# Expert dispatch: weights loaded in 1 KB runs and put in tile order by block transposes, first input tile loaded by strided partition sets

## The chip, the core and the metric

The kernel runs on one core of a Trainium2 chip. The metric is the device time of one execution in microseconds, as the median of several runs. One execution was also profiled, and its trace is what the prediction reads.

## What is computed

Each token's row of 512 numbers is written twice, once times each of the token's two expert weights. The expert indices are an input that the result does not use.

```python
batch, seq, hidden, k = 16, 1024, 512, 2
x_expanded = x[:, :, np.newaxis, :].repeat(k, axis=2)
return (x_expanded * expert_weights[..., np.newaxis]).astype(np.float32)
```

All is float32: 33.55 MB of x and 0.13 MB of weights are read, 67.11 MB are written.

## The kernel before

The 16384 tokens are taken in 8 tiles of 2048. In a tile, partition p holds 16 tokens that follow one another in memory, so that one partition's row of x is 16 x 512 numbers, 32 KB in one run. Tiles of x go through a pool of two buffers, output tiles through a pool of four.

**Weights.** One SBUF tile `w_tile` of 128 x 256 holds all of them: column (tile x 16 + token) x 2 + expert. It is filled by eight DMAs on SP's queue (lines 54 and 55), one for each tile of x; each writes 32 numbers, 128 bytes, to each of 128 partitions.

**Loads of x.** `load(i)` (lines 69 to 77) issues one DMA of 4 MB on ACT's queue, of 128 rows of 32 KB (line 76). Tiles 0 and 1 are loaded ahead of the loop. Tile i+2 is loaded after the compute of tile i, into the buffer that tile i leaves; it waits until DVE and ACT have read that.

**Compute.** For each of the 16 tokens of a partition, DVE multiplies 128 x 512 by the first weight (line 97) and ACT by the second (line 91). The weight is a column of `w_tile`, one number per partition.

**Stores.** After every 8 tokens SP issues one DMA of 4 MB (line 105), of 128 rows of 32 KB. There are 16 of them. Weight loads and stores stand in one queue (SP's, q1 in the profile), loads of x in another (ACT's, q10).

The order of the work is that of the program on each engine and queue. Waits on tiles are put in by the framework. It also shares out eight semaphores among the DMAs in turn, so that a DMA can wait for an older one that used the same semaphore: the second load of x waits for the first weight load, the eighth weight load for the first load of x, and the first stores for weight loads.

Of the kernel before, what the change touches and what calls it, by code (L numbers as in the profile page):

```python
# [1 line left out]

# [4 lines left out]


@with_exitstack
def kernel(  # L10
    ctx: ExitStack,
    tc: tile.TileContext,
    x: bass.AP,
    expert_indices: bass.AP,
    expert_weights: bass.AP,
    out: bass.AP,
):
    nc = tc.nc

    batch, seq, hidden = x.shape  # L20
    k = expert_weights.shape[-1]
    P = nc.NUM_PARTITIONS
    ntok = batch * seq
    assert ntok % P == 0
    A_TOTAL = ntok // P

    f32 = mybir.dt.float32
    row = k * hidden
    TX = 16
    TO = 8  # L30


    groups = [[16], [16], [16], [16], [16], [16], [16], [16]]
    assert sum(sum(g) for g in groups) == A_TOTAL

    xf = x.rearrange("b s h -> (b s) h")
    of = out.rearrange("b s k h -> (b s) (k h)")
    wf = expert_weights.rearrange("b s k -> (b s) k")

    w_pool = ctx.enter_context(tc.tile_pool(name="w_pool", bufs=1))  # L40
    x_pool = ctx.enter_context(tc.tile_pool(name="x_pool", bufs=2))
    o_pool = ctx.enter_context(tc.tile_pool(name="o_pool", bufs=4))

    w_tile = w_pool.tile([P, A_TOTAL * k], f32)

    def rows(of_all, done, T):
        return of_all[done * P : (done + T) * P, :].rearrange(
            "(p a) n -> p (a n)", a=T
        )

    weights = []
    for group in groups:
        weights.append((sum(n for _, n in weights), sum(group)))
    for at, T in weights:
        nc.sync.dma_start(out=w_tile[:, at * k : (at + T) * k], in_=rows(wf, at, T))

    tiles = []
    done = 0
    for group in groups:
        T = sum(group)  # L60
        a0 = 0
        for n in group:
            tiles.append((done, T, a0, n))
            a0 += n
        done += T

    loaded = []

    def load(i):
        if i >= len(tiles):  # L70
            return
        done, T, a0, n = tiles[i]
        x_tile = x_pool.tile([P, TX * hidden], f32)
        cols = rows(xf, done, T)[:, a0 * hidden : (a0 + n) * hidden]
        for lo, hi in [(0, P)]:
            nc.scalar.dma_start(out=x_tile[lo:hi, : n * hidden], in_=cols[lo:hi, :])  # L76
        loaded.append(x_tile)

    for i in range(2):
        load(i)  # L80
    for i, (done, T, a0, n) in enumerate(tiles):
        x_tile = loaded[i]
        outr = rows(of, done, T)
        for t in range(n):
            if t % TO == 0:
                o_tile = o_pool.tile([P, TO * row], f32)
            for kk in range(k):
                c = (done + a0 + t) * k + kk
                o = t % TO * row + kk * hidden
                if kk == 1:  # L90
                    nc.scalar.mul(  # L91
                        out=o_tile[:, o : o + hidden],
                        in_=x_tile[:, t * hidden : (t + 1) * hidden],
                        mul=w_tile[:, c : c + 1],
                    )
                    continue
                nc.vector.tensor_scalar(  # L97
                    out=o_tile[:, o : o + hidden],
                    in0=x_tile[:, t * hidden : (t + 1) * hidden],
                    scalar1=w_tile[:, c : c + 1],  # L100
                    scalar2=None,
                    op0=mybir.AluOpType.mult,
                )
            if (t + 1) % TO == 0:
                nc.sync.dma_start(
                    out=outr[:, (a0 + t + 1 - TO) * row : (a0 + t + 1) * row],
                    in_=o_tile,
                )
        load(i + 2)

# [1 line left out]
_INS = ['x', 'expert_indices', 'expert_weights']  # L112
_OUTS = [((16, 1024, 2, 512), 'float32')]


# [23 lines left out]
```

## Time and profile before

| | us |
|---|---|
| median of 11 runs | 240.28 |
| lowest and highest run | 240.06, 241.75 |
| profiled execution, its own time | 241.75 |
| its span in the trace | 240.0 |
| DVE busy | 51.9 (128 multiplies of 480 ns) |
| ACT busy | 81.3 (128 multiplies of 708 ns, one table load of 1283 ns) |
| first load of x, issue to landing | 12.8 |
| first weight load, issue to landing | 3.0 |
| all eight weight loads, median to landing | 21.7 |

The profile's page gives the span in 40 slices of 6 us with the share of DMA time and the GB/s of each slice; the busy time of each engine; the DMAs by the line that issues them; and groups of instructions with what ended the idle time before them. The trace can be asked for the same by windows of any length. It also holds a record of every DMA packet: when it began, how long it took, its bytes and its queue, but not its DMA engine; where the prediction speaks of single engines, packets were put in 16 chains, each packet behind the one that ended just before it.

The profile's whole-kernel figures are 100.81 MB moved in 240.0 us, 420 GB/s on average.

### The profile page before, as it was taken

Reading aid. Unit: us, or ns where it says so; the run is one execution under the profiler, and the core shown is the slowest. Engines: PE = TensorE matmul, PEld = TensorE weight load, DVE = VectorE, ACT = ScalarE, POOL = GpSimd, SP = SyncE. Lnnn points to the kernel's source line nnn. Section 1 sums busy time; section 2 is a strip of 40 time slices with the busy share of each in tenths; the row PEclk is TensorE's granted clock in tenths of the full one; section 3 lists DMA queues with packets and bytes.
Section 4 is the critical chain, followed back from the end, with each engine's and each line's share of the span. In section 5 each row is a group of like instructions: output and inputs, shape, how many; then the busy total and the mean of one; then the engine's idle time right before and its main releaser. Section 6 shows DMA issues by size and latency. Waiting matters only on the chain.

```text
span 240.0 us, 384 instructions
## 1 busy us (share of the span) xinstructions
DVE 51.9 (22%) x128; ACT 81.3 (34%) x129; POOL 0.2 (0%) x4
## 2 busy tenths in 40 slices
DVE  0073810055005005050040502205041135000000
ACT  2079870085207108071170802508044165200000
POOL 0000000000000000000000000000000000000000
DMA  6999999999999999999999999999999999999994
GB/s 265 439 433 364 438 437 437 432 437 426 432 426 415 418 415 426 426 437 437 432 432 432 426 437 432 426 426 432 437 437 437 437 437 437 437 432 437 437 432 197
DMA packets 4610, 100.81 MB, mean 420 GB/s; under 512 B 1536, under 2 KB 1536, under 8 KB 1536
## 3 DMA queue, kind: packets, MB, share of 16 engines
q1 hardware_dynamic: 3456, 67.24, 65.2%
q10 hardware_dynamic: 1152, 33.55, 33.2%
q14 instruction: 2, 0.02, 0.0%
HBM read 33.69 MB, written 67.11 MB: 420 GB/s over the span
## 4 chain that ended last, share of the span: by engine, by line
DMA 48%; another core or an unknown queue 21%; ACT 16%; ACTq 1%; issue 1%
DMA out_dram<-o_tile 38%; ACT o_tile L91 16%; DMA x_tile<-in_x_dram 9%; DMA w_tile<-in_expert_weights_dram 1%; ACTq L76 1%; ACTq L134 0%; ACTq L91 0%
## 5 line engine op out<-in xcount | busy, mean ns | idle before, releaser
L91 ACT ACTIVATE o_tile<-x_tile,w_tile 128x512 f32<-128x512 f32 x128 | 80.0, 708 | 120.0 <-DMA out_dram<-o_tile 97.0
L97 DVE TENSOR_SCALAR o_tile<-x_tile,w_tile 128x512 f32<-128x512 f32 x128 | 51.9, 480 | 151.9 <-DMA out_dram<-o_tile 116.5
L91 ACT ACT_TABLE_LOAD x1 | 1.3, 1283 | 4.2 <-DMA w_tile<-in_expert_weights_dram 4.2
L123 POOL MEMSET const-bfloat16-1.0<- 128x1 bf16 x1 | 0.1, 102 | 0.0
L123 POOL MEMSET const-uint8-127<- 128x1 uint8 x1 | 0.1, 102 | 0.0
L123 POOL MEMSET const-float32-0.0<- 128x1 f32 x1 | 0.1, 99 | 0.2 <-issue 0.2
L123 POOL MEMSET const-float32-1.0<- 128x1 f32 x1 | 0.1, 99 | 0.0
## 6 DMA issues: line engine op xcount, KB each, us to landing
out_dram<-o_tile SPq DMA_DIRECT2D x16, 4096.0 KB, 48.7
x_tile<-in_x_dram ACTq DMA_DIRECT2D x8, 4096.0 KB, 23.1
w_tile<-in_expert_weights_dram SPq DMA_DIRECT2D x8, 16.0 KB, 21.7
```

The lines of the kernel that those rows point to most:

```text
L76: nc.scalar.dma_start(out=x_tile[lo:hi, : n * hidden], in_=cols[lo:hi, :])
L91: nc.scalar.mul(out=o_tile[:, o : o + hidden], in_=x_tile[:, t * hidden : (t + 1) * hidden], mul=w_tile[:, c : c + 1],)
L97: nc.vector.tensor_scalar(out=o_tile[:, o : o + hidden], in0=x_tile[:, t * hidden : (t + 1) * hidden], scalar1=w_tile[:, c : c + 1], scala ...
L123: nc = _bacc.Bacc("TRN2", target_bir_lowering=False, num_devices=1)
```

## The change

**Weights.** One DMA on SP's queue reads all weights in memory order: 128 rows of 256 numbers, 1 KB each, into `w_in`. In that order partition p holds the weights of tokens 128p to 128p + 127. Two steps on DVE bring them into the tile order of before: a transpose of the 32 x 32 blocks of the whole 128 x 256 tile into `w_mid`, then 16 transposes of 32 partitions x 64 numbers, which read `w_mid` with strides and write the blocks of `w_tile` at their partitions.

**First tile of x.** It is loaded by four DMAs on ACT's queue, of partitions 0, 8, 16, ... (16 rows), 4, 12, 20, ... (16 rows), 2, 6, 10, ... (32 rows) and 1, 3, 5, ... (64 rows). All other tiles are loaded as before.

The loops over groups of tiles are written out for the one group length in use; multiplies and stores are the same in number, shape and order. With fewer DMAs at the start, the second load of x waits for no weight load any more. ACT's table load, which came after a wait for the first weight load, now comes after a wait for the four DMAs of the first tile.

```diff
-    wf = expert_weights.rearrange("b s k -> (b s) k")
+    wf = expert_weights.rearrange("b s k -> (b s k)")
...
-    w_tile = w_pool.tile([P, A_TOTAL * k], f32)
...
-    for at, T in weights:
-        nc.sync.dma_start(out=w_tile[:, at * k : (at + T) * k], in_=rows(wf, at, T))
...
+    w_in = w_pool.tile([P, R * C], f32)
+    w_mid = w_pool.tile([P, R * C], f32)
+    w_tile = w_pool.tile([P, G * C], f32)
+    nc.sync.dma_start(out=w_in, in_=wf.rearrange("(p n) -> p n", p=P))
+    nc.vector.transpose(out=w_mid, in_=w_in)
+    GQ = G // (P // B)
+    for dst in range(P // B):
+        for src in range(P // B):
+            nc.vector.transpose(
+                out=w_tile[
+                    dst * B : (dst + 1) * B, src * GQ * C : (src + 1) * GQ * C
+                ],
+                in_=w_mid[src * B : (src + 1) * B, :].rearrange(
+                    "c (q g h j) -> c g h j q", q=R, g=GQ, h=P // B
+                )[:, :, dst],
+            )
...
     def load(i):
-        if i >= len(tiles):
+        if i >= G:
             return
-        done, T, a0, n = tiles[i]
         x_tile = x_pool.tile([P, TX * hidden], f32)
-        cols = rows(xf, done, T)[:, a0 * hidden : (a0 + n) * hidden]
-        for lo, hi in [(0, P)]:
-            nc.scalar.dma_start(out=x_tile[lo:hi, : n * hidden], in_=cols[lo:hi, :])
+        if i == 0:
+            for at, step in ((0, 8), (4, 8), (2, 4), (1, 2)):
+                nc.scalar.dma_start(
+                    out=x_tile[at::step, :], in_=rows(xf, i)[at::step, :]
+                )
+        else:
+            nc.scalar.dma_start(out=x_tile, in_=rows(xf, i))
         loaded.append(x_tile)
```

Here P = 128, B = 32, G = 8 tiles, C = 32 weights of a partition in a tile, R = 8.

More of the change, by code (lines that the diff above doesn't have):

```diff
@@ L30 @@
     TO = 8
-    groups = [[16], [16], [16], [16], [16], [16], [16], [16]]
-    assert sum(sum(g) for g in groups) == A_TOTAL
+    G = A_TOTAL // TX
+    C = TX * k
+    B = 32
+    R = 8
+    assert A_TOTAL % TX == 0 and C == B and G * (P // B) == B and A_TOTAL * k == R * B
     xf = x.rearrange("b s h -> (b s) h")
     of = out.rearrange("b s k h -> (b s) (k h)")
-    wf = expert_weights.rearrange("b s k -> (b s) k")
+    wf = expert_weights.rearrange("b s k -> (b s k)")
     w_pool = ctx.enter_context(tc.tile_pool(name="w_pool", bufs=1))
@@ L42, with rows @@
     o_pool = ctx.enter_context(tc.tile_pool(name="o_pool", bufs=4))
-    w_tile = w_pool.tile([P, A_TOTAL * k], f32)
-    def rows(of_all, done, T):
-        return of_all[done * P : (done + T) * P, :].rearrange(
-            "(p a) n -> p (a n)", a=T
-        )
-    weights = []
-    for group in groups:
-        weights.append((sum(n for _, n in weights), sum(group)))
-    for at, T in weights:
-        nc.sync.dma_start(out=w_tile[:, at * k : (at + T) * k], in_=rows(wf, at, T))
[L57 to L65, printed above, removed]
+    def rows(of_all, g):
+        return of_all[g * P * TX : (g + 1) * P * TX, :].rearrange(
+            "(p a) n -> p (a n)", a=TX
+        )
+    w_in = w_pool.tile([P, R * C], f32)
[14 more added lines that the diff above has]
+            )
     loaded = []
     def load(i):
-        if i >= len(tiles):
+        if i >= G:
             return
-        done, T, a0, n = tiles[i]
         x_tile = x_pool.tile([P, TX * hidden], f32)
-        cols = rows(xf, done, T)[:, a0 * hidden : (a0 + n) * hidden]
-        for lo, hi in [(0, P)]:
-            nc.scalar.dma_start(out=x_tile[lo:hi, : n * hidden], in_=cols[lo:hi, :])
+        if i == 0:
[5 more added lines that the diff above has]
+            nc.scalar.dma_start(out=x_tile, in_=rows(xf, i))
         loaded.append(x_tile)
@@ L80 @@
         load(i)
-    for i, (done, T, a0, n) in enumerate(tiles):
+    for i in range(G):
         x_tile = loaded[i]
-        outr = rows(of, done, T)
-        for t in range(n):
+        for t in range(TX):
             if t % TO == 0:
@@ L87 @@
             for kk in range(k):
-                c = (done + a0 + t) * k + kk
+                c = i * C + t * k + kk
                 o = t % TO * row + kk * hidden
@@ L95 @@
                     )
[L96 to L103, printed above, removed]
+                else:
+                    nc.vector.tensor_scalar(
+                        out=o_tile[:, o : o + hidden],
+                        in0=x_tile[:, t * hidden : (t + 1) * hidden],
+                        scalar1=w_tile[:, c : c + 1],
+                        scalar2=None,
+                        op0=mybir.AluOpType.mult,
+                    )
             if (t + 1) % TO == 0:
                 nc.sync.dma_start(
-                    out=outr[:, (a0 + t + 1 - TO) * row : (a0 + t + 1) * row],
+                    out=rows(of, i)[:, (t + 1 - TO) * row : (t + 1) * row],
                     in_=o_tile,
```

## The prediction

> **What bounds the kernel now.** I read the page's slices first, then its DMA issues, then the trace by short windows around the places where the DMA rate falls, then the packet records there (start, length, size and queue of every DMA packet).
>
> The page, slices and DMA issues:
>
> ```profile
> span 240.0 us, 384 instructions
> ...
> DMA  6999999999999999999999999999999999999994
> GB/s 265 439 433 364 438 437 437 432 437 426 432 426 415 418 415 426 426 437 437 432 432 432 426 437 432 426 426 432 437 437 437 437 437 437 437 432 437 437 432 197
> ...
> out_dram<-o_tile SPq DMA_DIRECT2D x16, 4096.0 KB, 48.7
> x_tile<-in_x_dram ACTq DMA_DIRECT2D x8, 4096.0 KB, 23.1
> w_tile<-in_expert_weights_dram SPq DMA_DIRECT2D x8, 16.0 KB, 21.7
> ```
>
> The DMA engines are busy in every slice; DVE and ACT work 22% and 34%. So the time is bytes over rate, plus what the DMA loses at the start, in the fourth slice (364), and at the end. Inputs and output are 3072 packets of 32 KB, 192 on each of 16 engines; nearly all take 1.213 us in the packet records. 192 x 1.213 = **232.9 us** that this change does not touch. The slowest engine ends its last packet at 238.81, so 5.9 us are start and stalls. The windows show where (columns: window, length, DVE, ACT and POOL busy with instructions begun, clock, DMA share, GB/s; a packet is booked whole where it starts, so single windows swing about 432):
>
> ```profile
> 1.00:2.00 1.00, 0.00 (x0) 0.00 (x0) 0.00 (x0) 1.00 0.66 173
> 2.00:3.00 1.00, 0.00 (x0) 0.00 (x0) 0.00 (x0) 1.00 0.93 334
> 3.00:4.00 1.00, 0.00 (x0) 0.00 (x0) 0.00 (x0) 1.00 0.87 361
> ...
> 21.00:22.00 1.00, 0.00 (x0) 1.00 (x3) 0.00 (x0) 1.00 1.18 296
> 22.00:23.00 1.00, 0.00 (x0) 1.00 (x3) 0.00 (x0) 1.00 0.06 8
> 23.00:24.00 1.00, 0.00 (x0) 0.47 (x1) 0.00 (x0) 1.00 1.66 567
> ```
>
> ```profile
> 4.00:13.00 9.00, 0.00 (x0) 1.28 (x1) 0.00 (x0) 1.00 1.00 428
> 13.00:22.00 9.00, 6.42 (x16) 8.44 (x14) 0.00 (x0) 1.00 1.06 413
> 22.00:24.00 2.00, 0.00 (x0) 1.47 (x3) 0.00 (x0) 1.00 0.86 287
> 24.00:76.00 52.00, 15.20 (x38) 22.30 (x36) 0.00 (x0) 1.00 1.01 434
> 76.00:90.00 14.00, 1.00 (x3) 2.76 (x5) 0.00 (x0) 1.00 1.00 408
> ```
>
> Two holes are to be seen. **The start:** packets begin 1.0 us after the issues at 0.72; the first x packet begins at 1.81 on the earliest engine, 2.37 on average, 3.43 on the last. **The hole at 22:** hardly a byte starts there. The packet records say why. A DMA engine takes packets of the two queues in turn, one for one: between 3.5 and 22.7 us the weights' 128-byte packets begin one behind each 32 KB packet of x. Of their 1024 packets, 688 are left when the second tile of x ends, and they run as a block from 22.7 to 25.2 us. No 32 KB packet starts from 21.72 to 23.30, and the 18 that start between 20 and 23 us take 1.99 us on average. The first store, issued at 18.60, stands behind the weights in the same queue.
>
> **The change, part by part.**
>
> (1) Eight weight loads of 128 packets of 128 bytes become one of 128 packets of 1 KB: 8 instead of 64 per engine, the same bytes. The 56 others go, and the block with them. From 13 to 24 us the DMA starts 9 x 413 + 2 x 287 = 4291 KB where 11 x 432 = 4752 would fit: 461/432 = **1.07 us**. It is on the path, since the queues have work waiting throughout. Bounds: 0.46 us if only the gaps ahead of the next 32 KB packet go (mean of the 16 engines); 1.98 us if the engine with the longest hole sets the end (its packet at 21.72 took 2.63, that is 1.42 over, and 0.56 of gap). I take 1.1, the windows' figure. SP also issues seven DMAs fewer, and its second store no longer waits for a weight load (6.1 us of SP's waits; issued at 25.11, its rows done at 23.47); worth nothing, as the first store's 9.7 us of packets lie ahead of it.
>
> (2) The first x load of 128 rows becomes four, of 16, 16, 32 and 64, so each engine's first row stands in a DMA of 16. Before, 256 first packets (128 of weights, 128 of x) are handed out over 1.73 to 3.43 us, 6.6 ns each; 144 (weights, and the first set) would take 0.96 us, so the last engine starts at about 2.7 instead of 3.43: **-0.7 us**. Bounds: nothing (the weights still come to it last), and -1.6 (all at 1.81). The three issues more on ACT's queue cost about 0.4 us each, from the first issue's 0.42; the second set is issued at about 1.1, the fourth at 2.0, each well before the engine's current row (1.2 us) and its successors are through. Cost nothing.
>
> (3) The second x load no longer waits for a weight load (before: issued at 3.79, 0.02 after the first weights landed). Nothing gained: the engines were with the first tile until 13.5.
>
> (4) On DVE stand 17 new transposes, one of 128x256 and 16 of 32x64, ahead of all else. The trace has none. By columns at the multiply's 480 ns per 512 they are 0.24 and 0.06 each, 1.2 us in all; if each took a whole 480 ns, 8.2 us. I take a fixed 0.10 (POOL's 128x1 MEMSET) plus the columns: 0.34 + 16 x 0.16 = 2.9 us, nearer the small rows. They wait for the weights, which landed at 3.77 before; done at 6.7, with 6 us of cover until x lands.
>
> (5) ACT's table load (1.28 us) waited for the first weights before, and lay under the load of x. Now the first wait of ACT's compute, placed ahead of it, is for the four x sets: it comes after them. x lands 0.3 us after the last engine's eighth packet (before: 3.43 + 8 x 1.22 = 13.2, landed 13.5); now 2.7 + 9.7 + 0.3 = 12.7. ACT starts at 14.0, its eight rows take 5.0 (8 x 0.626), the first store is issued at 19.0 and its packets begin 1.0 to 2.7 us later (as at the start), 20.0 to 21.7. The second tile of x ends on the engines at 21.4 to 22.1 (16 x 1.213 behind their starts). So (4) and (5) cost **nothing**, with 0.4 to 1.4 us in hand; whatever comes later than that is lost one for one.
>
> (6) The steady part, the buffers and the end stay: between 24 and 205 us there is no gap for the compute to fill.
>
> Sum, against the profiled execution: 241.75 (span 240.0 and 1.75 around it) - 1.1 - 0.7 = 239.95. That execution is 1.47 above the median of 240.28; 14 x (432 - 408)/432 = 0.8 us of that is the slow stretch from 76 to 90 us, which the change does not touch. So the median goes to 240.28 - 1.8 = **238.5**. No engine can do better than 1.81 + 232.9 + 1.16 (last packet to the end of the span) + 1.75 = 237.6.
>
> [...]
>
> **The rivals.**
>
> A, slower: strided sets run at half rate. Every row of before is written by a DMA of all 128 partitions; none has 16 of them. Packets doubled from 1.213 to 2.43 (packets of 1.8 to 2.6 us do occur, at 1.8 and at 21 us) cost 1.21 us each: two for the first two sets, 238.5 + 2.4 = 240.9, about no change; with the third set's two 243.3; with all eight 248.2. Slower by over 0.3% from 2.5 us on, a mean of 1.53 us over the eight packets. Against it: when all engines work on rows of their own, 1.213 holds throughout.
>
> B, the weights land late. If x's first rows are ahead, the weights' eight packets and the semaphore's go one for one behind x packets, as the later weight loads did (the second, issued at 1.16, landed at 16.0): landing at 9.5 to 12.9, transposes done at 12.4 to 15.8. Against the 14.0 that ACT needs, that is up to 1.8 late and 1.4 lost: 239.9. With transposes at their upper bound, 8.2 us, some 6 are lost: 244.5. Against it: the first weight load was through on each engine before its first x packet.
>
> C, it doesn't do what it says: the long packets at 21 us belong to the change from loads to stores, and the start is set elsewhere. Then only some of the gap goes: 240.0. Against it: the third tile's x packets, between stores, take 1.213.
>
> **How the numbers follow.** Forecast 238.5, own range 237.5 to 239.4: 0.68. B at 239.9: 0.10, of which a quarter still faster; C at 240.0: 0.08; A with two sets: 0.05; A with more, or B at its upper price: 0.09. A difference under 0.3% (0.72 us) can't be told from no change here. Faster 0.71, same 0.20, slower 0.09. The range goes from the floor to C and A's mild case, 237.4 to 240.9.
>
> **What would show it.** (1) right: no window near 8 GB/s around 22 us, and 13 to 24 us at 430. (2) right: more than 173 and 334 GB/s in the second and third us, x landing before 13. A: those windows fall, x lands at 15 or later. B: DVE's first multiply is released by its transposes, not by x, and the first store comes after 20 us. (5): a table load of 1.28 us right behind x's landing. Wrong altogether if the steady rate changes, or a hole opens between the second tile and the first store.

## The result

The changed kernel takes 241.91 us (median of 13 runs, 241.29 to 242.90) against 240.20 of the kernel before (50 runs, 239.97 to 241.75): a ratio of 1.0067, 95% interval 1.0052 to 1.0082. It is 1.7 us slower, clear of the noise, where 1.7 us faster was forecast. Its profiled execution took 242.30 us, with a span of 240.5.

The page of the changed kernel: slices, groups of instructions, DMA issues.

```profile
span 240.5 us, 398 instructions
...
GB/s 196 349 436 436 436 431 387 436 425 439 436 420 425 436 436 436 436 431 436 436 436 436 431 436 431 420 436 436 436 425 436 436 436 436 431 425 436 436 436 240
...
L101 ACT ACT_TABLE_LOAD x1 | 1.3, 1283 | 15.8 <-DMA x_tile<-in_x_dram 15.8
L65 DVE STREAM_TRANSPOSE w_tile<-w_mid 32x64 f32<-32x64 f32 x16 | 4.4, 276 | 0.3
L61 DVE STREAM_TRANSPOSE w_mid<-w_in 128x256 f32<-128x256 f32 x1 | 0.4, 445 | 2.8 <-DMA w_in<-in_expert_weights_dram 2.8
...
x_tile<-in_x_dram ACTq DMA_DIRECT2D x1, 2048.0 KB, 13.1
x_tile<-in_x_dram ACTq DMA_DIRECT2D x2, 512.0 KB, 6.3
x_tile<-in_x_dram ACTq DMA_DIRECT2D x1, 1024.0 KB, 8.9
w_in<-in_expert_weights_dram SPq DMA_DIRECT2D x1, 128.0 KB, 2.1
```

The weights land after 2.1 us and the transposes are done at 7.9, long before x. The fourth slice, 364 GB/s before, is whole. But the first two slices read 196 and 349 where before had 265 and 439, and the seventh, from 36 to 42 us, reads 387 where before had 437. The same trace by windows, the first fence over the first packets, the second over the stretches that the prediction used (columns as there):

```profile
2.00:3.00 1.00, 0.18 (x1) 0.00 (x0) 0.00 (x0) 1.00 2.48 617
3.00:4.00 1.00, 0.94 (x4) 0.00 (x0) 0.00 (x0) 1.00 0.15 33
4.00:5.00 1.00, 0.96 (x4) 0.00 (x0) 0.00 (x0) 1.00 2.08 459
5.00:6.00 1.00, 0.94 (x5) 0.00 (x0) 0.00 (x0) 1.00 0.15 33
```

```profile
4.00:13.00 9.00, 3.73 (x14) 0.00 (x0) 0.00 (x0) 1.00 1.00 346
13.00:22.00 9.00, 6.15 (x16) 6.17 (x9) 0.00 (x0) 1.00 0.97 419
22.00:24.00 2.00, 0.28 (x1) 2.00 (x5) 0.00 (x0) 1.00 1.10 475
24.00:76.00 52.00, 12.84 (x32) 22.72 (x37) 0.00 (x0) 1.00 1.00 427
```

In what follows an engine is one of the 16 DMA engines, where no other is named, and a row is one packet of 32 KB, to or from one partition. In the first fence nearly all engines start a row, then one engine in a microsecond, then nearly all again: the rounds are 2.2 to 2.4 us apart. In the packet records the first row of each engine takes 2.21 us on average, the second 2.37 (2.34 to 2.42 on all 16), the third 1.85, all others of that tile 1.21 to 1.22. The DMA share stays at 1.00 over 4 to 13 us while the rate is 346: the engines are busy, only slow. From 13 to 24 us there is no hole (429 GB/s over the two windows). The timeline shows what follows from x:

```profile
15.81 1.28 ACT L101 ACT_TABLE_LOAD   x1 [15.81 <-DMA x_tile<-in_x_dram]
15.85 6.42 DVE L107 TENSOR_SCALAR o_tile<-x_tile,w_tile 128x512 f32<-128x512 f32 x16 [7.93 <-DMA x_tile<-in_x_dram]
17.11 10.52 ACT L101 ACTIVATE o_tile<-x_tile,w_tile 128x512 f32<-128x512 f32 x17
22.14 15.02 SPq L115 DMA_DIRECT2D out_dram<-o_tile  x4
```

x is there at 15.7 instead of 13.5, the table load stands right behind it, and the first store goes out at 22.14. The engines do not run dry: the second tile's rows last until 25.

For a sum I use one measure throughout, worked out from the packet records: **lost time**, the time passed less the rows moved so far (1.213 us each, those under way in part), as a mean over 16 engines. The lost time at 235 us, 232.9 us of rows, the time by which the last engine ends after the mean engine, and the time from the last packet to the end add up to the span. The trace of before shown above was of a run 1.5 us over the median, so the second trace of it, of a run of 240.02 (f1 below), is set beside it.

| trace, and its run's time | lost at 20 | at 24 | at 45 | at 235 us | last engine after mean | after last packet |
|---|---|---|---|---|---|---|
| before, f1, 240.02 | 2.76 | 4.09 | 4.05 | 3.75 | 0.44 | 1.16 |
| before, first trace, 241.75 | 2.84 | 4.14 | 4.14 | 4.59 | 1.33 | 1.16 |
| changed, 242.30 | 5.15 | 5.16 | 5.88 | 5.61 | 0.63 | 1.39 |
| e1, weights alone, 240.85 | 2.92 | 3.10 | 4.03 | 3.80 | 1.16 | 1.21 |
| e2, sets alone, 242.20 | 5.21 | 5.22 | 5.63 | 5.32 | 0.82 | 1.39 |
| e4, sets of 32, 32, 64, 241.51 | 2.94 | 3.27 | 4.15 | 4.14 | 1.39 | 1.30 |
| f4, weights, table load early, 240.74 | 2.82 | 3.87 | 3.87 | 3.57 | 1.21 | 1.27 |
| h4, weights, third load later, 240.11 | 2.90 | 2.90 | 3.50 | 3.33 | 0.91 | 1.19 |

Changed against f1: +2.39 by 20 us (the sets), -1.32 from 20 to 24 (nothing is lost there any more), +0.76 from 24 to 45, +0.03 after, +0.19 for the last engine, +0.23 at the end: 2.28, and the spans differ by 2.27.

### The profile page after: what moved, and what is told of

Same layout as the page of the kernel before. It is cut to its first block, busy times and chain, and to the rows that moved or that the text cites. A ratio compares the mean times of both kernels' runs of the same rounds, so it can differ in the third digit from the quotient of the medians.

```text
span 240.5 us, 398 instructions
## 1 busy us (share of the span) xinstructions
DVE 56.7 (24%) x145; ACT 81.0 (34%) x129; POOL 0.2 (0%) x4
## 4 chain that ended last, share of the span: by engine, by line
DMA 65%; ACT 12%; another core or an unknown queue 7%; ACTq 1%; issue 1%
DMA out_dram<-o_tile 39%; DMA x_tile<-in_x_dram 26%; ACT o_tile L101 12%; ACTq L83 1%; ACT L101 1%; ACTq L87 0%; ACTq L144 0%; ACTq L101 0%
## 5 line engine op out<-in xcount | busy, mean ns | idle before, releaser
L65 DVE STREAM_TRANSPOSE w_tile<-w_mid 32x64 f32<-32x64 f32 x16 | 4.4, 276 | 0.3
```

Source lines behind the costliest of these rows:

```text
L65: nc.vector.transpose(out=w_tile[dst * B : (dst + 1) * B, src * GQ * C : (src + 1) * GQ * C], in_=w_mid[src * B : (src + 1) * B, :].rearrange(
```

## The experiments

**What makes the first rows long.** Three theories: P, the partitions that a set names, every eighth in the first two, which make its rows take about twice 1.213 us; T, the transposes and 1 KB runs beside them; H, reading every eighth row of HBM.

e1, the weights of the change alone (the edit is to the changed kernel):

```diff
-        if i == 0:
-            for at, step in ((0, 8), (4, 8), (2, 4), (1, 2)):
-                nc.scalar.dma_start(out=x_tile[at::step, :], in_=rows(xf, i)[at::step, :])
-        else:
-            nc.scalar.dma_start(out=x_tile, in_=rows(xf, i))
+        nc.scalar.dma_start(out=x_tile, in_=rows(xf, i))
```

> The new weights (one DMA of 1 KB runs, transposes) with the first tile of x as one DMA of 128 rows. [...] Rival T (the rows are long because DVE's transposes and the 1 KB packets run beside them, 2.8 to 7.9 us): the first three rows of each engine stay at 1.9 to 2.4 us, x lands near 15.7, median near 241.9. [...]

Measured: 241.41 us, ratio 1.0043 (1.0028 to 1.0059). The second row of each engine is back at 1.213 to 1.220, x lands at 13.4, the hole at 22 us is gone: so far P (or H), and not T. But the time is 1.2 us above before, not 1.1 below, as step (1) of the prediction had it: this part of the forecast fails by itself. Its timeline:

```profile
9.70 0.45 DVE L61 STREAM_TRANSPOSE w_mid<-w_in 128x256 f32<-128x256 f32 x1 [9.70 <-DMA w_in<-in_expert_weights_dram]
10.18 4.63 DVE L65 STREAM_TRANSPOSE w_tile<-w_mid 32x64 f32<-32x64 f32 x16
13.39 1.28 ACT L94 ACT_TABLE_LOAD   x1 [13.39 <-DMA x_tile<-in_x_dram]
14.69 10.52 ACT L94 ACTIVATE o_tile<-x_tile,w_tile 128x512 f32<-128x512 f32 x17
```

Here the weights land at 9.7, half of their packets one for one behind x, and the transposes end only at 14.8, after x. Yet no DMA engine waits for that: lost time rises by 0.18 us from 20 to 24.

e2, the sets alone, with the weights of before in one DMA, since the sets would else wait for semaphores of weight loads (the edit is to the kernel before):

```diff
-    for at, T in weights:
-        nc.sync.dma_start(out=w_tile[:, at * k : (at + T) * k], in_=rows(wf, at, T))
+    nc.sync.dma_start(out=w_tile[:, :].rearrange("p (g n) -> p g n", g=len(groups)),
+        in_=wf.rearrange("(g p a) k -> p g (a k)", g=len(groups), p=P))
...
-        for lo, hi in [(0, P)]:
-            nc.scalar.dma_start(out=x_tile[lo:hi, : n * hidden], in_=cols[lo:hi, :])
+        if i == 0:
+            for at, step in ((0, 8), (4, 8), (2, 4), (1, 2)):
+                nc.scalar.dma_start(out=x_tile[at::step, :], in_=cols[at::step, :])
+        else:
+            nc.scalar.dma_start(out=x_tile[:, : n * hidden], in_=cols)
```

> The strided sets of 16, 16, 32 and 64 with the old weights (128-byte runs straight into tile order, no transposes; all in one DMA, so that no set waits for a semaphore of a weight load). P and H: second row of each engine at 2.36 us as in the changed kernel, third near 1.9, x lands near 15.7; median 240.2 + 2.4 to + 3 = 242.6 to 243.2, more if the weights, 64 packets on an engine, go one for one behind x and hold up the first store. T: rows at 1.213, x lands near 13, median 239 to 240.3.

Measured: 242.32 us, 1.0087 (1.0070 to 1.0105). Second rows at 2.36 to 2.40, third at 1.4 to 2.1, with no transpose in the kernel, and x is there when ACT's table load starts:

```profile
15.81 1.28 ACT L96 ACT_TABLE_LOAD   x1 [15.81 <-DMA x_tile<-in_x_dram]
```

T is out. The weights in one DMA are not the cause either: e5 below has them without the sets, and its second rows take 1.21 to 1.28 us.

e3, the changed kernel with blocks of neighbours instead of strided sets:

```diff
-            for at, step in ((0, 8), (4, 8), (2, 4), (1, 2)):
+            for lo, hi in ((0, 16), (16, 32), (32, 64), (64, 128)):
```

> The changed kernel with the sets as blocks of neighbours: partitions 0 to 15, 16 to 31, 32 to 63, 64 to 127, neighbouring rows in HBM. [...] H: rows at 1.213, since the HBM rows are neighbours, x lands near 12.7, time near 239. T: as the changed kernel, near 241.9.

Measured: 255.95 us (one run). The rate by windows (last column GB/s), and then, from the timeline, the moment when x is there:

```profile
4.00:13.00 9.00, 3.07 (x11) 0.00 (x0) 0.00 (x0) 1.00 0.95 124
13.00:20.00 7.00, 1.78 (x7) 0.00 (x0) 0.00 (x0) 1.00 0.92 192
20.00:24.00 4.00, 0.00 (x0) 0.00 (x0) 0.00 (x0) 1.00 0.92 188
```

```profile
29.01 1.28 ACT L101 ACT_TABLE_LOAD   x1 [29.01 <-DMA x_tile<-in_x_dram]
```

Rows take 3.75 and 4.47 us in the two blocks of 16, then 3.29 and 2.41 to 2.56 in those of 32 and 64. Neighbouring HBM rows do not help, so H is out; 124 and 188 to 192 GB/s are a bit over a quarter and a bit under half of 432. Of the three that leaves P, the partitions: rows to 16 neighbours take longer still than rows to every eighth (4.47 us against 2.37). Why is not shown.

e4, the changed kernel with no set of 16:

```diff
-            for at, step in ((0, 8), (4, 8), (2, 4), (1, 2)):
+            for at, step in ((0, 4), (2, 4), (1, 2)):
```

> The changed kernel with sets of 32, 32 and 64 (every fourth partition from 0, from 2, every second from 1): no set of 16. [...] H: rows every fourth are half as bad, first rows near 1.8, median 240 to 241. T: as the changed kernel, 241.9.

Measured: 241.51 us, 1.0044 (1.0023 to 1.0065). No long second row (1.21 us, to every fourth partition), x at 13.4: P again. But it is like e1 (241.41), not faster than before, and starting with a set of 32 rows wins nothing: the first rows begin at 2.40 on average, against 2.46 in e1, 2.36 in the changed kernel, and 2.18 in f1.

**Where the weights' gain went.** e1 against f1 in the table: 0.99 us better at 24 us, then 0.97 worse by 45 (+0.93 against -0.04), and the last engine 0.72 further behind the mean. The windows show the second of these:

f1 (before):

```profile
20.00:24.00 4.00, 0.00 (x0) 2.96 (x5) 0.00 (x0) 1.00 0.98 286
24.00:34.00 10.00, 6.42 (x16) 9.93 (x16) 0.00 (x0) 1.00 0.98 423
34.00:42.00 8.00, 0.00 (x0) 0.00 (x0) 0.00 (x0) 1.00 1.05 455
```

e1 (weights alone):

```profile
20.00:24.00 4.00, 2.00 (x6) 4.00 (x8) 0.00 (x0) 1.00 1.00 410
24.00:34.00 10.00, 5.68 (x15) 10.00 (x17) 0.00 (x0) 1.00 1.00 429
34.00:42.00 8.00, 0.00 (x0) 0.40 (x1) 0.00 (x0) 1.00 1.00 381
```

286 becomes 410, but 455 becomes 381, about the end of the first store's packets, while the third tile of x is loaded: about a third of the rows of x take 1.3 to 2.5 us there (33 to 45 us) in e1, e2, e4 and the changed kernel, none in f1.

f1, before once more, unchanged:

> The kernel before, unchanged, for a second trace: the first one was of a run 1.5 us above the median. Theory Q (the weights alone do save the 1.0 us of the block at 22 us, and lose it again where x packets are long near the first store's end, at 35 to 41 us, and where a few DMA engines fall behind the rest): a run near 240.2 shows the block at 22 us (lost time up by 1.3 us a DMA engine between 20 and 24), no long x packets later, and its engines ending within 0.6 us. Rival R (the block at 22 costs a typical run nothing): the block is small or missing in a run of 240.2.

Measured: 240.02 us. The block is there in an ordinary run (2.76 to 4.09), with no long rows from 24 to 45 us, and the engines end within 0.83 us (236.26 to 237.09; Q had 0.6). R is out, and Q stands for this trace; f4 below corrects what it says of the block. The slow stretch from 76 to 90 us in the first trace is not here: it belonged to that run.

e5, the kernel before with its 128-byte runs in one DMA (the first hunk of e2 alone):

> The kernel before with its 128-byte runs all in one DMA: no transposes, no 1 KB runs, x in one DMA of 128 rows. If the weights' packets go ahead of x (as in the run with sets and 128-byte runs), there is no block at 22 us. Theory Q: then the long packets at 35 to 41 us come here too, and the median is 240.9 to 241.5 though no transpose is there. Rival S (the new time comes from transposes and 1 KB runs themselves): median 239.0 to 239.5.

Measured: 249.36 us, 1.0374 (1.0341 to 1.0407). It does not tell Q and S apart, since the weights came too late:

```profile
23.47 1.28 ACT L93 ACT_TABLE_LOAD   x1 [23.47 <-DMA w_tile<-in_expert_weights_dram]
23.50 12.76 DVE L99 TENSOR_SCALAR o_tile<-x_tile,w_tile 128x512 f32<-128x512 f32 x32 [23.50 <-DMA w_tile<-in_expert_weights_dram]
```

By 3.5 us 448 of the DMA's 1024 packets had begun, 28 an engine; 16 an engine then went one for one behind rows of x, and the last 20 only when the second tile was through, from 22 to 23 us. The first store went out at 29.8, and the engines stood idle for 8.3 us on average. In e2, where the sets' rows (each issue 0.60 us) came to the engines later, 960 had begun by 3.5 us, and all by 5.4.

f3, e1 with three output tiles instead of four:

```diff
-    o_pool = ctx.enter_context(tc.tile_pool(name="o_pool", bufs=4))
+    o_pool = ctx.enter_context(tc.tile_pool(name="o_pool", bufs=3))
```

> Weights alone with three output tiles instead of four, so that the fourth store (issued at 34.4, just ahead of the long packets) can only be issued after the first has landed, at 40 or later. If the fourth store's issue makes the x packets long, they are at 1.213 from 34 to 40 us and the median falls to 240.2 to 240.6; if the first store's end does, they stay at 1.4 to 2.5 and the median stays near 241.4.

Measured: 242.18 us, 1.0077 (1.0049 to 1.0105), rows of 1.4 to 1.7 us still at 35 us, so the fourth store's issue does not make them. New: two engines ended at 239.0 and 239.2, 3 us after the middle one.

f4, e1 with the table load brought forward:

```diff
+    warm = w_pool.tile([P, 2], f32)
+    nc.gpsimd.memset(warm, 1.0)
...
+    nc.scalar.mul(out=warm[:, 1:2], in_=warm[:, 0:1], mul=warm[:, 0:1])
```

> Weights alone, with ACT's table load brought forward by a one-column multiply ahead of the wait for x: the first store goes out 1.28 us sooner, near 18.4. If ACT's late start costs anything, the median falls by up to 1.2 us, to 240.2; Theory Q: the DMA engines had no gap there (nothing idle from 19 to 24 us), so it stays within 0.4 of 241.4.

Measured: 240.94 us, 1.0033 (1.0012 to 1.0055); runs from 239.98 to 242.26. The first store at 18.48 is 1.25 us earlier, the median 0.5 lower than e1's; the two intervals overlap. The trace shows what was not looked for. The last weight packet begins at 6.9 us, and still the hole at 22 us is back (by windows):

```profile
20.00:24.00 4.00, 0.07 (x1) 3.35 (x6) 0.00 (x0) 1.00 0.88 279
22.00:23.00 1.00, 0.00 (x0) 1.00 (x3) 0.00 (x0) 1.00 0.15 66
```

Lost time rises by 1.05 us from 20 to 24, against 1.33 in f1 and 0.18 in e1. What is long is the last row of the second tile of x, 2.14 us on average. In f1 it takes 2.05, which is 0.84 us over 1.213, out of the 1.33; the gaps in which the block of weight packets runs make the other 0.48. So most of that hole needs no weight packets. It goes with the moment of the first store. Among the traces with the first tile there by 13.0 to 13.6 us and the weights in time, the last row of the second tile takes

| first store issued at | traces | last row of the second tile, mean |
|---|---|---|
| 18.1 to 18.6 us | both of before, f4 | 2.05 to 2.14 us |
| 19.6 to 19.8 | e1, e4, g1, g2, h2 | 1.40 to 1.69 |
| 20.0 to 20.2 | f3, g3, h1, h4 | 1.21 to 1.24 |

and in the changed kernel, with the store at 22.14 and its second tile's last rows beginning at 23.4 instead of 21.0, it takes 1.22. e1 and f4 differ in the table load, which holds up e1's first store: with the later store the long rows are mostly gone, with the early one they are back, and f4 has hardly a long row at 33 to 45 us (0.04 us an engine; 0.91 in e1). Why an early store makes these rows long is not shown.

At this point the packets, put in chains by engine, showed another difference (two chains can be mixed up where packets end within 0.02 us of each other, so the counts at the start are surer than which engine ends last). In f1 all 16 engines make 4 stores before their first row of the third tile, in e1 3 make 5 and 13 make 6, in f4 10 make 5 and 6 make 6, in f3 15 make 6 and one makes 7. From this came theory V: the moment at which the third load reaches the engines splits them, and those out of step are slowed. The next runs are e1 with an ACT multiply into a spare tile ahead of the third load; it delays that load, and with it ACT's rows of the second tile and their stores:

```diff
+        if i == 0:
+            nc.scalar.mul(out=spare[:, 0:N], in_=x_tile[:, 0:N], mul=w_tile[:, 0:1])
         load(i + 2)
```

g1, N = 256:

> Weights alone, with the third load of x issued about 0.4 us later, by one extra ACT multiply of 256 columns into a spare tile behind the first tile's compute. Theory V (the 16 DMA engines fall into two groups: those that have started 5 stores when the third tile's rows arrive and those that have started 6, and the split makes long packets and late engines): the arrival moves out of the stretch in which the engines' store packets begin, all 16 make the same number of stores first, packets over 1.213 after 24 us add up to under 0.3 us an engine instead of 1.13, engines end within 0.6 us; median 239.3 to 239.9. Rival W (the second store and the third load are issued in the same 0.01 us, and that makes the long packets): gone too, median 239.3 to 239.9. Rival Z (the moment of the third load does not matter): median stays near 241.4.

g3, N = 736:

> The same with 736 columns, a delay of about 0.8 us, two thirds of a packet. V: at the edge of the good stretch (first stores begin over 0.66 us, which leaves 0.55 of 1.21): split in some runs, median 239.5 to 241. W: 239.3 to 239.9. Z: 241.4.

g2, N = 1216:

> The same with 1216 columns, a delay of about 1.2 us, the length of one packet. V: the engines are split as in weights alone, long packets return, median 240.9 to 241.6. W: the issues are apart, so it is as good as with 0.4 us, 239.3 to 239.9. Z: 241.4.

Measured, with the third load's issue (24.63 in e1): g1 at 25.09, 242.68 us, 1.0055 (1.0022 to 1.0087); g3 at 25.80, 240.34, 0.9996 (0.9965 to 1.0026), runs from 239.66 to 242.48; g2 at 25.83, 240.39, 0.9990 (0.9970 to 1.0009). From g1 to g2, whose first stores went out at 19.78 and 19.73, the moment moves the median by 2.3 us (their intervals do not overlap), so Z is out; g1 has the issues 0.4 us apart and is the worst, so W is out. V's own numbers did not hold: it had 0.4 us as the good delay and 1.2 as the bad one. In g3 the first store moved too (20.09). In the traces, all 16 engines make 7 stores first in g3 (run of 239.66, the lowest of all), 9 make 6 and 7 make 7 in g2, 15 make 6 and one makes 5 in g1. The end of g1 by windows shows that one:

```profile
236.00:237.00 1.00, 0.00 (x0) 0.00 (x0) 0.00 (x0) 1.00 0.08 33
237.00:238.00 1.00, 0.00 (x0) 0.00 (x0) 0.00 (x0) 1.00 0.08 33
238.00:239.00 1.00, 0.00 (x0) 0.00 (x0) 0.00 (x0) 1.00 0.08 33
```

One packet of 32 KB starts in each microsecond: a single engine works alone, to 240.02, when the other 15 have ended by 236.7. It is the one with 5 stores. Its long packets lie at 36 (2.39 us), 61, 78 (2.31), 89, 120 and 143 us. f1, in the same place, has nothing left to start:

```profile
236.00:237.00 1.00, 0.00 (x0) 0.00 (x0) 0.00 (x0) 1.00 0.01 0
```

g4, the changed kernel with N = 512:

> The changed kernel with its third load of x about 0.6 us later, by one extra ACT multiply of 512 columns. In the changed kernel 2 engines make 5 stores before the third tile, 13 make 6 and 1 makes 7. V and W: one group, less than 0.3 us of long packets after 24 us, median 241.9 - 0.7 to - 1.0 = 240.9 to 241.2; what stays above 240.2 is the sets' 2.4 us less the block's 1.3. Z: 241.9.

Measured: 242.32 us, 1.0063 (1.0038 to 1.0088). Not lower than the changed kernel, V's number missed again. Long rows at 33 to 45 us fell from 0.67 to 0.13 us an engine, but others came later (0.49 after 95 us).

Further traces, for the relation of count and lag. h1 (g3 again), h2 (e1 again), h3 (the changed kernel again), h4 (N = 960):

> The kernel with the third load 0.8 us later, once more for another trace: its runs went from 239.66 to 242.48. Theory V, narrowed (the time is set by the last of the 16 DMA engines, and an engine that makes one store more or less than most before the third tile's rows falls 1 to 4 us behind): if all 16 make the same number, the last engine ends within 1.0 us of the middle one and the run is at 239.6 to 240.0; if one or a few differ, the last engine is one of them and the run is at 240.7 to 242.5; if they fall in two halves, it is between. Rival Z: the last engine's lag has nothing to do with the count.

> Weights alone once more, for another trace (runs of 240.85 to 241.53): V: split again, some engines with 5 stores and most with 6, the last engine one of the few, 1.0 to 1.6 us behind the middle one. Z: no such relation.

> The changed kernel once more (runs of 241.29 to 242.9). V: the lost time at 20 us is 5.1 to 5.2 us an engine again (the sets), no rise from 20 to 24 us, and what differs from the first trace is how many engines are out of step and how far the last one lags: 0.5 us of lag at 241.9, 1.5 at 242.9. Z: the lost time at 20 us itself differs.

> Weights alone with the third load about 1.0 us later (960 columns), between the runs with 0.8 (median 240.34, half its runs under 240.4) and 1.2 (240.39, two groups of 9 and 7). V: two uneven groups or one, median 239.7 to 241.0, and its trace keeps to the relation of count and lag. If one group were to come out in nearly all runs, 239.7, it would beat both kernels by 0.2%. Z: 240.4, no relation.

Measured: h1 240.60 us, all 16 with 7 stores, and still one engine 1.2 us after the middle one, against V. h2 240.39, below all five runs of e1, with 8 engines at 5 stores and 8 at 6, lag 0.9: one run of the weights alone that is only 0.2 us above before. h3 243.37, 14 with 6 and 2 with 5, the last engine 1.9 behind, and whether it is one of the two is not sure; lost time at 20 us 5.04 (5.15 in the first trace), so the runs of the changed kernel differ in the later part, not in the sets (V, not Z). In its first trace 3 engines were out of step and the lag was only 0.48. h4 240.22 us, 0.9985 (0.9961 to 1.0010), runs only from 239.97 to 240.40; in its trace all 16 with 7. Its windows:

```profile
20.00:24.00 4.00, 3.41 (x10) 4.00 (x8) 0.00 (x0) 1.00 1.01 434
24.00:34.00 10.00, 5.47 (x14) 10.00 (x17) 0.00 (x0) 1.00 0.99 419
34.00:42.00 8.00, 0.00 (x0) 1.83 (x3) 0.00 (x0) 1.00 0.97 393
```

So the new weights can be as fast as the old ones and as even, but no version tried beats the kernel before by more than the measurement can tell. What of V is shown: the moment of one later load, with the rows behind it, moves the median by 2.3 us; and in g1, f3 and h3 the kernel's end is that of one to four late engines. Not shown: that the count decides the lag (h1 and the first trace of the changed kernel speak against that), and why rows of x are long around 35 us, which they are, less so, in h4 as well.

## Why the prediction was wrong

- **Step (2), the sets, is the step that failed first.** It put them at -0.7 us. They cost +2.4 us by 20 us. The first rows do not begin sooner: at 2.36 us on average against 2.18 in f1, the last of them at 2.85 against 2.86; the 3.43 that the step wanted to save was one engine of one run. The issues took 0.60 us each, not 0.4. And the first three rows take 2.21, 2.37 and 1.85 us where 1.213 was reckoned, 2.8 us more in all. Part of that is not the sets': a first row is long in f1 too (1.68 on average) and in e1 and e4 (1.54 and 1.79), while their second rows take 1.21 to 1.23.
- **Rival A came true in its mild form**, two rows near twice 1.213 and a third of 1.85, begun while other engines were still at their second. Its price of 2.4 us for the rows was right; its chance was put at 0.05. The row against it (1.213 whenever all engines work) came from loads of 128 rows, and the rival itself said that none of these has 16.
- How long a row takes went with the partitions of its DMA. Every eighth: 2.37 us (second rows of the changed kernel), 1.95 times 1.213. 16 neighbours: 4.47 us (e3), 3.7 times; 32 or 64 neighbours: 2.4 to 2.6 behind a first one of 3.29 (e3). Every fourth: 1.85 and then 1.21 (the changed kernel), 1.213 (second rows of e4); every second: 1.21 to 1.22 (the last four rows of the changed kernel's first tile). No run shows by what mechanism.
- **Step (1), the weights' block, gave the hole to the wrong cause.** The stretch from 20 to 24 us did come out clean (1.1 forecast; 1.33 lost in f1, 0.01 in the changed kernel), and the step's sign, 13 to 24 us at 430 GB/s, was met (429). But of the 1.33 the block's gaps are 0.48, the lower bound of 0.46 that the step named and passed over, and 0.84 are long rows. f4, which has the new weights and an early store, loses 1.05 there without a weight packet. Rival C's reason, the change from loads to stores, is thus right for most of the hole. The changed kernel, with its late store, lost nothing there, so the 1.1 was met by luck.
- **Step (6), "the steady part stays", failed too.** Weights alone gave back 0.97 us in long rows by 45 us and 0.72 in the last engine's lag, and e1 came out at +1.2 us (h2, one run, at +0.2). "It is on the path, since the queues have work waiting throughout" holds; but the time is that of the last engine, and what comes after the start changed. The runs of before, from 240.06 to 241.75, and the slow stretch that the prediction itself took out were signs that the steady part is not fixed.
- Step (3) held. Step (4): the transposes take 5.1 us (2.81 to 7.92; 0.45 and 16 of 0.276 with gaps), not 2.9, under their upper bound of 8.2, and were covered. Rival B's late weights did come in e1 (9.7 us), without cost, and in e5, for 9 us. Step (5) held: the table load stands behind x, and the first store came without a gap on the engines; no row of the first trace showed that the store's moment also goes with how long rows are.
- The sum, by the traces of the changed kernel and f1: the sets +2.39 instead of -0.7, the stretch to 24 us -1.32 instead of -1.1, and +1.21 after it (0.76, 0.03, 0.19, 0.23) that the prediction put at nothing: 4.1 us in all. The two runs lie 0.4 us above and 0.2 below their medians, which leaves, to 0.1 us, the 3.4 between 241.91 and 238.5.
- The parts do not add. Weights alone are at +1.2 us (e1), sets alone at +2.1 (e2), both together at +1.7.

## What to carry to other kernels

Before a transfer is cut by partitions, measure how long a row takes in each kind of piece: here the second rows, to every eighth partition, took 2.37 us where those of one DMA of 128 rows took 1.213 to 1.220 (e1), and the first ones did not even start sooner (2.36 us on average against 2.18 in f1). Before a hole is priced, split it into rows that are long and gaps between rows, and see whether it is still there when the supposed cause is gone: here most of it was (1.05 us of lost time from 20 to 24 us in f4, 1.33 in f1). Where the DMA bounds a kernel, as here, its time is that of the last DMA engine (g1: one at 240.02 us, the other 15 by 236.7): work out each engine's end, not only the mean rate. Time saved at the start can be lost again later (e1: 0.99 us ahead of f1 at 24 us, 0.02 at 45), so it is worth trying when the next load and the first store are issued before a gain is written off or claimed.

## What was not expected of the hardware

- A DMA engine out of step with the others can end 3.8 us after the middle one with the same number of packets (g1: 240.02 against 236.24).
- An ACT multiply of 1.08 us ahead of one load (issued at 26.06 us in h4, 24.63 in e1) went with a time 1.2 us lower and even runs (e1 241.41, 1.0043; h4 240.22, 0.9985), though one more run of e1's kernel beside h4 took 240.39.
- The last row of the second tile took 2.05 to 2.14 us when the first store was issued at 18.1 to 18.6 us, and 1.21 to 1.24 when it was issued at 20.0 to 20.2.
- A DMA of a strided set took 0.55 to 0.62 us to issue, one of a block of neighbours 0.41 to 0.53, one of 128 rows 0.42 at the start and 0.33 later; but one of 128 rows right behind the four sets took 0.62 as well.
- The same weight DMA landed at 2.8 us in the changed kernel, where all its 128 packets had begun by 2.4 us, and at 9.7 in e1, where 64 of them were left behind rows of x. A first load of 16 rows does not decide it: beside blocks of neighbours (e3) it landed at 9.8.
